# Earlier norm transposes, earlier weights, rotation before value split and stacked queries by transfer in a one-core encoder layer

## The chip, the cores and the metric

The kernel runs on one core of a Trainium2 chip. The metric is the device time of one launch in microseconds, over a few runs. A profile is one execution on the chip. In it PE is TensorE's matrix multiplication, PEld its weight load, DVE the vector engine, ACT the scalar engine, POOL GpSimd, and SP the engine that does nothing but issue transfers. A "q" behind an engine's name is its sequencer, where it issues transfers or waits. "L269" is line 269 of the kernel before.

## The reference

One encoder layer over 1024 tokens of width 1024. Two kinds of attention share one input norm and one input projection:

```python
hn = rmsnorm(h, norm_mix)
proj = hn @ w_in                      # 1024 x 2304
qa, ka, va, qb, kb, vb = split(proj)  # A: 8 query heads, 2 key/value heads; B: 8 heads
qa, ka = partial_rope(qa, cos, sin), partial_rope(ka, cos, sin)   # 16 of 64 dims
o_a = window_gqa_sink(qa, ka, va, sink)       # |i-j| <= 128, a learned sink
o_b = neighbourhood_attention(qb, kb, vb, rpb)  # 8 x 16 window on a 16 x 64 grid
mix = concat(rmsnorm(o_a, norm_a), rmsnorm(o_b, norm_b))
h = h + mix @ w_out
hn = rmsnorm(h, norm_ffn)
h = h + (silu(conv3(hn @ w_gate) + conv_b) * (hn @ w_up)) @ w_down
return rmsnorm(h, norm_final)
```

The change touches only the first norm, the projection's first tiles, the rotation and the layout of group A's queries.

## The kernel before

Everything lies transposed: features on the 128 partitions, the 1024 tokens along the row. Matrix products are made nearly exact by splitting each operand into a high part and the rest: one 128 x 128 block of weights against 512 tokens takes three matmuls (`block`, L171 to L174). Weights are loaded raw, ACT rounds them to the high part (`halve_w`, L156), and DVE, or POOL in some stages, subtracts to get the low part (L157).

The input projection has 18 tiles of 128 columns, made in the order m = 0 to 17. Tiles 0 to 5 belong to group A in two groups of three: the first tile of a group (m = 0 and 3) holds a 64-row key head and its 64-row value head, the two others hold four query heads. The tiles 0 and 1 (`first`) are computed straight from the incoming input, the third (m = 2, `third`) behind them from its own weights. The input is used without its norm: each product is scaled by the row factor `rstd1` when it leaves PSUM (`evacuate`, L269).

`rstd1` is made so: ACT squares the eight input tiles and DVE adds them into `acc` (L211, L213). `inverse_power` turns 4 blocks of `acc` on PE (L221), DVE sums them (L223), scales and adds epsilon (L224), and POOL raises to the power of minus one half (L225). `widen` (L263) turns the result back on PE, broadcast over the partitions, and ACT copies it out (L772). This is done once for each half of the tokens. In between lie the scans: ACT sums the squares of the eight output weight tiles (`scan_out`, L755 and L756), which are needed for a scale much later.

After the evacuation, `turn` treats a group A tile. `rotate` (L277 to L292) sends the rows to be rotated out by two transfers, one from ACT and one from SP, into a folded layout (L285), does four DVE operations (L287 to L289) and sends the rows back by two SP transfers (L291). For a group's first tile, `split_v` also takes the largest absolute value of each value row (L357), forms scales from it (L358 to L362), and makes two half precision parts, the high one on ACT (L374), the rest on DVE (L375); these are then turned by a transposing transfer (L378).

`stacks` then builds the operands of the score products, two tiles a and b each with a high part in one half of the partitions and a rest in the other. There are two ways for queries. `split_first` (L305) computes every quarter in its place: two ACT operations (L309) and two DVE operations (L310), each on 64 rows. `split_pair` (L294) computes the high part of all 128 rows at once on ACT (L297) and the rest on DVE (L299), and three SP transfers of 64 rows bring them across (L300 to L302), the third of which overwrites rows that the first reads. `split_first_k` does the keys of the first group with L316 to L319. Before the change the first group's two query tiles both use `split_first`, the second group's both use `split_pair`.

The attention itself works in units of 128 queries. For each head PE makes scores (L432), DVE adds the mask and finds the maximum (L462), ACT takes the exponential (L466), and the result is turned, partly by PE (L494, copied out by L497 and L498), partly by a transposing transfer (L488, a flip), and multiplied with the values (L521). Between these steps PE works on the remaining projection tiles: `rest` is a generator that gives one block at a time, and `fill(n)` takes n of them. `FILL0 = 22` blocks, the 16 of the fourth tile and 6 of the fifth, come ahead of the first score.

What sets the order of the work:

- PE is scheduled by hand: its instructions run in the order in which the program writes them.
- On DVE, ACT, POOL and SP a planner lays out the order from when an instruction becomes ready in its own model and from its place in the program. `tc.high_priority(offset=...)` moves a passage up. `behind(name)` puts what is written in it behind a marked instruction of the same engine. Once laid out, each engine serves its queue strictly in order.
- The stacks of the first two tiles are written behind "copied", the evacuation of the fourth tile's first half. The fifth tile's second half of weights is written behind "stack" (the last ACT half of the second tile's stacks), with its low part on POOL. The third tile's stacks come behind those weights.
- Tiles come from pools with a fixed number of slots. Raw weights have two slots, so a load waits until an earlier raw tile was halved.

In `turn` the order of the two calls and the name of the loop variable matter:

```python
g, i = divmod(m, 3)
if i == 0:
    (v,), up = split_v(t, slice(64, 128))
    va[g] = v
    for i in range(2):
        scaled_gain(2 * g + i, up, C_NA + 2 * g + i)
rotate(t, 64 if i == 0 else 128, ["back"] * (m in (1, 2)))
```

## Time and profile before

| what | value |
|---|---|
| median of 3 runs | 1039.76 us (1037.07 to 1040.96) |
| span of the profiled execution | 1035.9 us; its time outside the span is not given |
| PE busy | 1011.7 us, 98% |
| DVE busy | 880.0 us, 85% |
| ACT busy | 679.3 us, 66% |
| POOL busy | 214.1 us, 21% |
| PE clock granted | 0.997 of full speed |
| first matmul of the input product / first score | 5.45 us / 62.29 us |

The profile's rows give a start, a duration and an instruction as "output <- inputs". A bracket at the end tells how long the engine was idle ahead of it and which instruction or transfer ended that. Matmuls overlap, so the time of one matmul is best read from the distance between two starts, not from its duration. The view of busy time by stretches gives, for each engine, busy microseconds and the number of instructions.

### The profile page before, as it was taken

To read this page: it belongs to the slowest core of one execution; us is meant where nothing else is said; L and a number is where in the kernel's file an instruction comes from. 1 tells how busy PE (TensorE), PEld (TensorE's weight loads), DVE (VectorE), ACT (ScalarE), POOL (GpSimd) and SP (SyncE) were. 2 spreads that over 40 slices of the span, in tenths; PEclk is the share of its full clock that TensorE was granted. 3 is DMA by queue.
4 is the path that set the end of the run, shared out by engine and by line. 5 is a ranking of instruction groups with operands and counts; after the bars stand their busy time and mean duration, and the time that the engine had idled before them with its cause. 6 is when DMAs were issued, how large, how long until landed. Compare 5 with 4: busy or idle time off the path is not lost.

```text
span 1035.9 us, 15696 instructions
## 1 busy us (share of the span) xinstructions
PE 1011.7 (98%) x5102; PEld 577.3 (56%) x5102; DVE 880.0 (85%) x1748; ACT 679.3 (66%) x1243; POOL 214.1 (21%) x341
## 2 busy tenths in 40 slices
PE   9998999999999999999999999999999999999996
PEld 7776777777775545544444444444444444444446
DVE  6699998766898699899898988888888879899875
ACT  8567787767687587645777777754535656655551
POOL 2235455676866301000000000000000000000002
PEclk9999999999999999999999999999999999999998
DMA  9447473676689775300687867733232778878744
GB/s 347 155 98 149 109 139 83 151 168 140 134 180 224 213 276 193 121 1 21 222 266 261 276 241 250 251 111 133 82 112 102 240 252 297 301 250 264 255 153 163
DMA packets 144275, 191.28 MB, mean 185 GB/s; under 512 B 77376, under 2 KB 88640, under 8 KB 144192
## 3 DMA queue, kind: packets, MB, share of 16 engines
q1 hardware_dynamic: 133536, 164.51, 54.7%
q10 hardware_dynamic: 10656, 25.76, 6.4%
q8 instruction: 40, 0.66, 0.2%
q14 instruction: 43, 0.35, 0.1%
HBM read 132.81 MB, written 28.57 MB: 156 GB/s over the span
## 4 chain that ended last, share of the span: by engine, by line
PE 71%; DVE 6%; ACT 1%; DMA 1%; issue 1%; POOL 0%; ACTq 0%; DVEq 0%; SPq 0%; POOLq 0%
PE dn L1177 6%; PE dn L1178 6%; PE dn L1176 6%; PE pj L180 6%; PE z L1176 5%; PE z L1177 5%; PE z L1178 5%; PE y L1176 4%; PE y L1177 4%; PE y L1178 4%; PE x L1176 4%; PE x L1177 4%; PE x L1178 3%; PE pj L172 2%; PE pj L174 2%; PE pj L173 2%
## 5 line engine op out<-in xcount | busy, mean ns | idle before, releaser
L1178 PEld LDWEIGHTS <-wlo 128*128 128x128 f16 x898 | 87.9, 98 | 101.3 <-DVE wlo L1151 0.2
L1176 PEld LDWEIGHTS <-whi 128*128 128x128 f16 x898 | 88.1, 98 | 100.3
L1177 PEld LDWEIGHTS <-whi 128*128 128x128 f16 x898 | 87.9, 98 | 100.3 <-issue 0.2
L1178 PE MATMUL dn<-xd,wlo 128*128 128x512 f16 (+1 forms) x330 | 120.4, 365 | 0.0
L1177 PE MATMUL dn<-xd,whi 128*128 128x512 f16 (+1 forms) x330 | 120.4, 365 | 0.0
L1176 PE MATMUL dn<-xd,whi 128*128 128x512 f16 (+1 forms) x330 | 120.4, 365 | 0.0
L172 PE MATMUL pj<-xgh,whi 128*128 128x512 f32 x248 | 106.8, 431 | 0.8 <-ACT whi L156 0.8
L1177 PE MATMUL z<-hg,whi 128*128 128x512 f16 x264 | 100.1, 379 | 0.0
L1178 PE MATMUL z<-hg,wlo 128*128 128x512 f16 x264 | 100.1, 379 | 0.0
L1176 PE MATMUL z<-hg,whi 128*128 128x512 f16 x264 | 100.1, 379 | 0.0
L466 ACT ACTIVATE p<-p,nm 128x385 f32<-128x385 f32 (+3 forms) x128 | 74.8, 585 | 38.0 <-DVE nm L462 33.3
L174 PE MATMUL pj<-xgh,wlo 128*128 128x512 f32 x248 | 97.9, 395 | 1.4 <-POOL wlo L157 1.4
L173 PE MATMUL pj<-xgl,whi 128*128 128x512 f32 x248 | 97.5, 393 | 0.0
L1150 ACT ACTIVATE whi<-ws,m 128x512 f16<-128x512 f32 (+1 forms) x96 | 65.9, 709 | 35.6 <-DVE ws L1317 19.5
L1151 DVE SCALAR_TENSOR_TENSOR wlo<-ws,m,whi 128x512 f16<-128x512 f32 (+1 forms) x96 | 70.2, 741 | 17.8 <-ACT whi L1150 17.6
L1031 POOL TENSOR_TENSOR back<-back,cst 128x4 f32<-128x4 f32 (+1 forms) x7 | 2.8, 396 | 356.7 <-DVE back L1030 356.7
L1165 ACT ACTIVATE scan<-scan 128x1024 f32<-128x1024 f32 (+1 forms) x60 | 61.1, 1019 | 17.0 <-DMA scan<-in_w_down_dram 12.3
L1150 ACT ACTIVATE whi<-raw,m 128x512 f16<-128x512 f32 (+1 forms) x78 | 51.4, 700 | 17.9 <-DMA raw<-in_w_down_dram 12.7
L1151 DVE SCALAR_TENSOR_TENSOR wlo<-raw,m,whi 128x512 f16<-128x512 f32 (+1 forms) x78 | 55.4, 732 | 7.5 <-ACT whi L1150 6.9
L1176 PE MATMUL y<-hg,whi 128*128 128x512 f16 x160 | 60.6, 379 | 0.0
L1177 PE MATMUL y<-hg,whi 128*128 128x512 f16 x160 | 60.6, 379 | 0.0
L1178 PE MATMUL y<-hg,wlo 128*128 128x512 f16 x160 | 60.6, 379 | 0.0
(291 smaller groups left out, 2465.5 us busy)
## 6 DMA issues: line engine op xcount, KB each, us to landing
xd<-x SPq DMA_DIRECT2D x77, 256.0 KB, 5.4
raw<-in_w_down_dram SPq DMA_DIRECT2D x64, 256.0 KB, 3.8
x<-c ACTq DMA_DIRECT2D x22, 512.0 KB, 3.5
scan<-in_w_gate_dram SPq DMA_DIRECT2D x18, 512.0 KB, 4.7
scan<-in_w_up_dram SPq DMA_DIRECT2D x18, 512.0 KB, 4.3
raw<-in_w_gate_dram SPq DMA_DIRECT2D x18, 512.0 KB, 3.8
raw<-in_w_up_dram SPq DMA_DIRECT2D x18, 512.0 KB, 4.4
raw<-in_w_in_dram SPq DMA_DIRECT2D x32, 256.0 KB, 3.1
```

The lines of the kernel that those rows point to most:

```text
L172: nc.tensor.matmul(ps, w[0], x[0][:, tsl(h)], start=first, stop=False)
L173: nc.tensor.matmul(ps, w[0], x[1][:, tsl(h)], start=False, stop=False)
L174: nc.tensor.matmul(ps, w[1], x[0][:, tsl(h)], start=False, stop=last)
L180: nc.tensor.matmul(ps, a, b, start=i == 0 and b is x[h][0] and a is w[0], stop=i == len(ws) - 1 and a is w[1])
L466: nc.scalar.activation(p[:, 0:e], p[:, 0:e], AF.Exp, bias=nm, scale=-1.0, accum_out=sm)
L1031: nc.gpsimd.tensor_tensor(back, back, unit_back.to_broadcast([128, n]), op=ALU.mult)
L1150: mark["whi"] = nc.scalar.activation(hi, src, AF.Copy, scale=by)
L1151: nc.vector.scalar_tensor_tensor(lo, src, by, hi, op0=ALU.mult, op1=ALU.subtract)
L1165: nc.scalar.activation(t, t, AF.Square, accum_out=dst)
L1176: nc.tensor.matmul(ps, w[0], x[0], start=first and i == 0, stop=False, skip_group_check=True)
L1177: nc.tensor.matmul(ps, w[0], x[1], start=False, stop=False, skip_group_check=True)
L1178: nc.tensor.matmul(ps, w[1], x[0], start=False, stop=last and i == len(ws) - 1, skip_group_check=True)
```

## The change

Four edits, all of them in the first 60 us of the program:

```diff
         def turn(m, t):
             g, i = divmod(m, 3)
             if i == 0:
+                rotate(t, 64)
                 (v,), up = split_v(t, slice(64, 128))
                 va[g] = v
                 for i in range(2):
                     scaled_gain(2 * g + i, up, C_NA + 2 * g + i)
-            rotate(t, 64 if i == 0 else 128, ["back"] * (m in (1, 2)))
+            else:
+                rotate(t, 128, ["back"] * (m in (1, 2)))
 
         def stacks(m, t):
...
-                qa[g, i - 1] = split_pair(t) if g else split_first(t)
+                qa[g, i - 1] = split_first(t) if m == 1 else split_pair(t)
...
         ps3 = [bank("s", "s") for _ in range(2)]
-        for _ in product(ps3[0], third.w, xg, 0):
-            pass
...
+        jobs[1].load()
+        jobs[1].load_rest()
         for d in range(KT):
             scan_out(d)
...
         rstd1 = big("rstd1", "rstd")
-        vs1 = [inverse_power(acc[:, tsl(h)], D, "pt") for h in range(2)]
-        rest3 = product(ps3[1], third.w, xg, 1)
-        for _ in range(3):
-            next(rest3)
-        for h in range(2):
-            nc.scalar.activation(rstd1[:, tsl(h)], widen(vs1[h], "pt"), AF.Copy)
+        rest3 = (step for h in range(2) for step in product(ps3[h], third.w, xg, h))
+        next(rest3)
+        v1 = gains
+        with tc.high_priority(offset=300):
+            for h in range(2):
+                sums1 = bank("st", "pt")
+                for c in range(4):
+                    nc.tensor.transpose(sums1[:, c * 128:(c + 1) * 128], acc[:, h * HALF + c * 128:h * HALF + (c + 1) * 128], ident)
+                nc.vector.tensor_reduce(v1[:, 4 * h:4 * h + 4], sums1[:, :].rearrange("p (c w) -> p c w", w=128), axis=mybir.AxisListType.X, op=ALU.add)
+            nc.vector.tensor_scalar(v1, v1, 1.0 / D, EPS, op0=ALU.mult, op1=ALU.add)
+            nc.gpsimd.tensor_tensor(v1, v1, minus_half[:, 0:1].to_broadcast([128, 8]), op=ALU.pow)
+            for _ in range(5):
+                next(rest3)
+            for h in range(2):
+                mark["root"] = nc.scalar.activation(rstd1[:, tsl(h)], widen(v1[:, 4 * h:4 * h + 4], "pt"), AF.Copy)
         for p, ps in zip(first, banks):
             p.t = tmp("t")
             for h in range(2):
                 evacuate(p.t, ps[h], h, False)
-            if p is first[0]:
-                jobs[1].load()
-                jobs[1].load_rest()
```

In words: both halves of the third tile's product become one stream of 16 steps. One step is written ahead of the norm's eight transposes, five between them and the widening, ten after; before it was eight ahead and three between. The two halves of the norm share one scaling, one power over eight columns and one buffer (`gains`, used later for something else). The fourth tile's two weight loads and their halving are written ahead of the scans. In `turn`, a group's first tile is rotated before its values are split, and over 64 rows. The third tile's query stacks are built by `split_pair`.

## The prediction

> **What bounds the kernel now.** I read the page first, then the busy time by stretches, then the timeline of each engine from 23 to 86 us, the list of waits, and the views of single lines.
>
> The span, and busy time by stretch (columns: PE, PEld, DVE, ACT, POOL, then granted clock, DMA share, GB/s):
>
> ```profile
> span 1035.9 us, 15696 instructions
> ```
>
> ```profile
> 50.00:75.00 25.00, 22.85 (x104) 18.38 (x104) 23.71 (x56) 14.18 (x27) 6.58 (x13) 1.00 0.38 94
> 75.00:100.00 25.00, 22.29 (x126) 16.33 (x125) 23.31 (x68) 19.09 (x48) 12.89 (x25) 1.00 0.76 150
> 100.00:125.00 25.00, 24.66 (x148) 18.85 (x146) 23.37 (x82) 19.34 (x51) 14.13 (x31) 1.00 0.53 120
> ```
>
> PE carries the kernel: from 100 us on it idles a third of a microsecond in 25. Before that, between 50 and 100 us, it is idle 4.9 us of 50 while DVE is busy 47. So there are two things to win: PE's waits themselves, and DVE work that now stands in front of PE. The order of PE's instructions is written by hand, so a microsecond taken out of PE's stream early moves all that follows, unless something else is late there. The order on DVE, ACT, POOL and SP is laid out by the planner from priorities and readiness.
>
> The waits, in PE's timeline (start, duration, instruction, idle before it and who ended it):
>
> ```profile
> 30.05 0.39 PE L172 MATMUL s<-xgh,whi 128*128 128x512 f32 x1
> ...
> 35.27 0.39 PE L174 MATMUL s<-xgh,wlo 128*128 128x512 f32 x1
> 35.50 1.03 PE L221 MATMUL st<-cst,sq 128*128 128x128 f32 x8
> 36.29 0.48 PE L172 MATMUL s<-xgh,whi 128*128 128x512 f32 x1
> ...
> 38.21 0.39 PE L174 MATMUL s<-xgh,wlo 128*128 128x512 f32 x1
> 39.03 0.65 PE L263 MATMUL sw<-cst,v 128*128 128x128 f32 x4 [0.43 <-POOL v L225]
> 40.70 0.65 PE L263 MATMUL sw<-cst,v 128*128 128x128 f32 x4 [1.01 <-POOL v L225]
> 41.10 0.47 PE L172 MATMUL s<-xgh,whi 128*128 128x512 f32 x1
> ...
> 57.99 0.39 PE L174 MATMUL pj<-xgh,wlo 128*128 128x512 f32 x1
> 59.15 0.50 PE L172 MATMUL pj<-xgh,whi 128*128 128x512 f32 x1 [0.78 <-ACT whi L156]
> 59.49 0.39 PE L173 MATMUL pj<-xgl,whi 128*128 128x512 f32 x1
> 61.26 0.50 PE L174 MATMUL pj<-xgh,wlo 128*128 128x512 f32 x1 [1.38 <-POOL wlo L157]
> ...
> 62.29 0.28 PE L432 MATMUL s<-ka,q 128*128 128x256 f32 x1
> ...
> 64.21 0.35 PE L432 MATMUL s<-ka,q 128*128 128x256 f32 x1
> ```
>
> From the first to the second row are 23 steps in 5.22 us: 0.227 us a matmul, 0.68 us a block of three. Measured from start to start, the four waits cost 0.82 - 0.23 = 0.6 (39.03), 1.67 - 0.40 = 1.27 (40.70; four widening transposes take 41.10 - 40.70 = 0.40), 1.16 - 0.23 = 0.93 (59.15) and 1.77 - 0.23 = 1.54 (61.26): 4.3 us. The first step behind a wait is longer too (59.49 - 59.15 = 0.34, 0.11 over), 0.4 for four. So **4.7 us** are lost before the first score matmul at 62.29. Counted forward it is the same: 114 matmuls of 0.227 and 16 transposes of 0.1 from 30.05 end at 57.5.
>
> **Part 1, the norm.** What feeds the widening now, from the timelines of DVE, POOL and ACT, and two views of lines with the power (count, then shortest, median, longest in ns):
>
> ```profile
> 28.09 2.54 DVE L213 TENSOR_TENSOR sq<-sq 128x1024 f32<-128x1024 f32 x2
> 36.13 1.29 DVE L223 TENSOR_REDUCE v<-st 128x4 f32<-128x512 f32 x2 [5.50 <-PE st L221]
> ...
> 42.02 0.69 DVE L269 TENSOR_TENSOR t<-pj,rstd 128x512 f32<-128x512 f32 x1 [0.97 <-ACT rstd L772]
> ```
>
> ```profile
> 35.59 0.99 POOL L554 TENSOR_TENSOR xb<-cst,rr 128x384 f32<-128x384 f32 x1 [9.72 <-DMA rr<-in_rpb_dram]
> 37.64 1.34 POOL L225 TENSOR_TENSOR v<-v,minus_half 128x4 f32<-128x4 f32 x1 [1.07 <-DVE v L224]
> ```
>
> ```profile
> L880 POOL TENSOR_TENSOR wo_by<-owm,minus_half x1: 580/580/580, 205.3 to 205.3; 128x1 f32<-128x1 f32 x1
> ```
>
> ```profile
> L225 POOL TENSOR_TENSOR v<-v,minus_half x6: 1017/1027/1566, 37.6 to 361.0; 128x4 f32<-128x4 f32 x6
> ```
>
> ```profile
> 34.75 1.14 ACT L156 ACTIVATE whi<-raw 128x512 fp32r<-128x512 f32 x2
> ```
>
> The sum of squares is done at 28.09 + 2.54 = 30.63, but its transposes stand behind 24 matmuls, so DVE sat idle 5.50 us. After the change they stand behind three: PE reaches them at 30.05 + 0.68 = 30.73, just after the sum. The eight transposes now span 36.29 - 35.50 = 0.8 us; both reduces are done near 32.5, the one tensor_scalar at 32.7. The power goes from four columns to eight: one column takes 0.58, four 1.03, so 0.15 a column more and about 1.63 for eight (ends: one power of four, 1.03, and two of the slowest, 3.13). That ends at 34.4 (33.8 to 35.9). PE needs it after five more blocks, 31.5 + 3.4 = 34.9. I take no wait; the far end makes it 1.0.
>
> ACT's last scan and the two copies L156 end at 34.75 + 1.14 = 35.9 in any order among themselves, so rstd1 comes at 36 to 37 and both evacuations of the first tile are done near 37.5 instead of 42.7. PE's third product ends at 30.05 + 48 x 0.227 + 1.6 = 42.5. The evacuations are thus hidden under PE's blocks: what they gain is room on DVE.
>
> **Part 2, the weights ahead of the scans.** Two loads and four half operations move, none is added. Now their DVE halves fill DVE's idle time before 40 us; with evacuations from 36.5 they must be gone by then. SP takes the two loads ahead of eight scan loads; nothing but a scale at 200 us waits for the scans. Cost nothing; if they stayed late, 1.4 us of DVE would fall between the evacuations, still under PE's blocks until 42.5.
>
> **Part 3, rotation ahead of the value split.** In the code before, the loop `for i in range(2)` in `turn` overwrites `i`, so the test `i == 0` behind it fails, and the first and fourth tile are rotated over all 128 rows, value rows included. Their transfers back (L291) write rows that the split (L375) still reads:
>
> ```profile
> 50.02 1.28 DVE L375 SCALAR_TENSOR_TENSOR vhl<-t,down,vhl 64x1024 f16<-64x1024 f32 x1
> ```
>
> ```profile
> 51.33 3.17 SPq L291 DMA_DIRECT2D t<-f  x4
> ```
>
> ```profile
> 54.13 1.06 ACT L316 ACTIVATE ka<-t 64x1024 fp32r<-64x1024 f32 x1 [5.55 <-DMA t<-f]
> ```
>
> L291 leaves at 51.33, 0.03 after L375 ends (51.30); SP serves in order, so the second and third tile's transfers back stand behind it, and ACT idles 5.55. After the change 64 rows are rotated, the split touches none of them, and the transfers leave after the last rotation add. An instruction's time goes by its columns, so the rotation's four DVE operations stay as long. First tile: evacuated 37.5, transfers out, four operations, back: K stacks possible from about 45 instead of 54.13. What is late next is the code's own order: the stacks' DVE halves are queued behind the evacuation of the fourth tile's first half, and PE gives that at 42.5 + 24 x 0.227 = 48.0, done 48.9. So of the 9 us on ACT some 6 reach DVE, and the early ACT halves bring the fifth tile's second weight half (ACT L156, then POOL L157, queued behind them) well ahead of PE's need. The two waits at 59.15 and 61.26 go, 2.5 us. For the fourth tile the same freedom is worth nothing: its stacks are used eight units later.
>
> **Part 4, the third tile's stacks by transfers.** `split_first` costs two ACT and two DVE operations of 64 rows, `split_pair` one of each over 128 rows and three transfers:
>
> ```profile
> 57.60 2.46 DVE L310 SCALAR_TENSOR_TENSOR q<-t,q 64x1024 fp32r<-64x1024 f32 x2
> ...
> 60.82 2.71 DVE L310 SCALAR_TENSOR_TENSOR q<-t,q 64x1024 fp32r<-64x1024 f32 x2
> ...
> 63.57 0.48 DVE L462 CUSTOM_DVE_ANT_0 p<-s,cst,nsink 128x256 f32<-128x256 f32 x1
> ...
> 66.86 1.22 DVE L357 TENSOR_REDUCE top<-t 64x1 f32<-64x1024 f32 x1
> ```
>
> ```profile
> L297 ACT ACTIVATE q<-t x2: 1042/1045/1048, 89.2 to 108.5; 128x1024 fp32r<-128x1024 f32 x2
> L300 SPq DMA_DIRECT2D q<-q x2: 462/523/584, 90.2 to 110.2; - x2
> L299 DVE SCALAR_TENSOR_TENSOR t<-t,q x2: 1224/1225/1226, 90.6 to 109.7; 128x1024 fp32r<-128x1024 f32 x2
> ```
>
> ```profile
> L302 SPq DMA_DIRECT2D q<-t x2: 466/786/1106, 94.0 to 113.4; - x2
> ...
> DMA to landing us min/median/max: 3.7/4.0/4.4
> ```
>
> DVE saves 2.71 - 1.22 = 1.5 and ACT 1.1. DVE's work is then 48.9, two K halves of 1.2, one L310 pair of 2.46, one evacuation of 0.69, L299 of 1.22: 55.7. The last transfer, L302, leaves with the next SP slot, 55.8 to 56.3, and lands 4.0 later: 60.1 (59.5 to 60.7). PE's first score comes at 62.29 - 4.7 = 57.6, the third, the first that reads these stacks, 64.21 - 62.29 = 1.92 behind it: 59.5. So PE waits 0.6 there (0 to 1.2). Behind that wait stand PE's next blocks and scores, and DVE, which has the fourth tile's value reduction (L357) to fill it. SP's own queue: the three transfers stand ahead of the sixth tile's weight loads and the fourth tile's rotation, half a microsecond each by L300's row.
>
> Against this part speaks the Trainium skill, "DMA: Bandwidth & Descriptors", section "Anatomy of one DMA": about 2.0 us fixed for each transfer plus its bytes at 436 GB/s, so 2.6 us for these 256 KB, an estimate from that page. The row has 3.7 to 4.4 for the same size, so the page's price is too low here; by the page the stacks would stand at 58.7 and the 0.6 would be nothing.
>
> **DVE's new room.** With PE at its first score at 57.6 and DVE done at 55.7, DVE is no longer late: at present its first softmax (63.57) starts the moment L310 ends (60.82 + 2.71 = 63.53), 0.9 after the scores. The 2 us between go to what now stands at 66.86 and after, the fourth tile's reduction and rotation, and these are what PE waits for at 80:
>
> ```profile
> 80.19 0.44 PE L494 MATMUL pt<-cst,p 128*128 128x128 f32 x2 [1.31 <-DVE turned L498]
> ```
>
> That wait I expect to go (ends: 0 to 1.3, and up to 2.7, PE's whole idle time between 75 and 100).
>
> **The sum.** -4.7 (four waits) + 0.6 (third score) - 1.3 (L494) = -5.4 us. Ends: -3.5 (third score 1.2, L494 stays) to -7.4 (no wait there, all idle time to 100 us gone). After 100 us nothing in the change acts directly; but the planner lays out other engines anew, and a changed order can cost or give waits like the one at 80.19; for two of them I add 2.5 to both sides. The profiled execution has a span of 1035.9 and what lies around it is not on the page; the three timed runs are 1037.07 to 1040.96, so 1.2 to 5.1 above it. I take the difference over to the median: 1039.76 - 5.4 = 1034.4. The forecast's own range is 1029.9 to 1038.8. Half a per cent, 5.2 us, is about what a measurement of this kernel can tell from no change, and the forecast sits on it.
>
> **Rivals.**
>
> *POOL's queue takes the gain of the norm.* POOL ran the bias tile L554 at 35.59, ahead of the power, when its load had landed. If the planner keeps that order, the power starts at 35.59 + 0.99 = 36.6 and ends at 38.2, and PE, in place of 1.9 us in two waits, has one of 38.2 - 34.9 = 3.3: the gain falls from 5.4 to 2.1: 1037.7 (1039.0 if the wait at 80.19 stays as well). For it: the row at 35.59, and one instruction cannot be passed in a queue. Against: the power now becomes ready at 32.7, about 3 us before that load landed, and has the priority. The Trainium skill, "TensorE: Matmul & The Clock Gate", section "What's actually happening", says that a pause of about 3.4 us halves the clock; no pause quoted here is longer than 1.6, and the granted clock is 1.00 in the rows above, so this trace cannot show it. By that rule this rival would lose another 1.7 us of gain, an estimate (3.4 us at half speed).
>
> *The stacks come late: slower.* The third tile's ACT half ran at 59.01 (the second L309 pair):
>
> ```profile
> 59.01 2.12 ACT L309 ACTIVATE q<-t 64x1024 fp32r<-64x1024 f32 x2
> ```
>
> If it stays there, because its rotation's transfers back are still late on SP, the chain L297, L300, L302 needs about 1.0 + 0.5 + 3.3 + 0.5 + 4.0 = 9.3 us (its 3.3 an estimate, L302 leaving 94.0 - 90.2 = 3.8 after L300): PE's third score at 68.3 instead of 64.21, 4.1 late, and all scores behind it: 1043.9; with a flip or a weight load ahead of L302 on SP, another 1.5, 1045.4. It decides from L297 starting after 64.21 - 9.3 = 54.9. Against: rotation of the third tile can start when PE's third product ends, 42.5 instead of 41.10 + 15 x 0.227 = 44.5, and nothing then holds SP; I get 51.
>
> *The gain is given back later.* From 100 to 340 us PE and DVE are both nearly full (the rows above: DVE 23.4 of 25). If DVE, not PE, sets the pace there and a new order costs it two waits of 1.3, the gain is 2.8 and the time 1037.0. For it: DVE's share; against: PE's idle 0.34 of 25.
>
> *The change does not act:* if the planner puts the stacks' ACT halves behind the same transfers as now, only the norm's 1.9 us are left: 1037.9.
>
> **How the numbers follow.** Forecast 0.72, POOL's queue 0.08, stacks late 0.08, given back 0.10, no action 0.02. Of the forecast's own range (1029.9 to 1038.8, middle 1034.4) somewhat over half lies below 1039.76 - 5.2 = 1034.56: 0.55 of 0.72 is 0.40, and 0.02 comes from the cases in which a rival's loss is met by a better order later: 0.42 faster. Slower than 1044.96 are the upper end of the late stacks (0.05), a new order that hits several waits at once (0.05): 0.10. The remainder, 0.48, is no change. Range: 1029.9 to 1039.5, which takes in the forecast and the three cases of a smaller gain and leaves out the late stacks and the tails, some 0.2.
>
> **What would show it.** In the new profile: the transposes L221's counterpart on PE at 30.7 and no wait at L263; first evacuation near 36.5; L291 near 42 and the first K stack's ACT half near 45; the weight waits at the fifth tile gone and its product unbroken; first score at 57.6; one ACT and one DVE operation of 128 rows for the third tile, the third score within 1.2 us of its turn; no 1.3 us wait for L498 near 75. Wrong if PE waits over 1 us at L263 (POOL's order), or at its third score (stacks), or if PE reaches 100 us of its old count early by 5 us and the end is early by less than 3 (given back).

## The result and the profile after

| | before | after |
|---|---|---|
| median of 13 runs each, us | 1038.97 (1037.07 to 1041.33) | 1037.12 (1035.60 to 1038.05) |
| ratio | | 0.9983, 95% interval 0.9975 to 0.9991 |
| span of the profiled execution, us | 1035.9 | 1035.1 |
| PE busy, us | 1011.7 | 1012.4 |

The change makes the kernel 0.17% faster (0.09 to 0.25%), 1.8 us where 5.4 had been forecast. The time lies within the range, the size of the gain does not fit its working.

One thing first for reading the two traces side by side. The third tile's first matmul, ahead of which the change touches nothing on PE, starts at 30.58 in the new profile and at 30.05 in the old. The 0.53 us between them are taken here as not the change's and are subtracted from the PE times of after: e2 below, which changes nothing ahead of that matmul either, has it at 30.69.

The busy time by stretches of after (columns as in the prediction):

```profile
span 1035.1 us, 15696 instructions
```

```profile
50.00:75.00 25.00, 20.50 (x89) 16.57 (x88) 22.03 (x50) 14.79 (x26) 5.73 (x10) 0.93 0.58 127
75.00:100.00 25.00, 23.63 (x133) 18.23 (x132) 20.74 (x66) 17.65 (x45) 12.78 (x26) 1.00 0.72 141
```

Between 50 and 75 us PE is idle 4.5 us, where it was 2.15 before, and the granted clock is 0.93, where it was 1.00. The PE timeline of after says where:

```profile
30.58 0.39 PE L172 MATMUL s<-xgh,whi 128*128 128x512 f32 x1
...
31.27 1.03 PE L776 MATMUL st<-cst,sq 128*128 128x128 f32 x8
...
35.57 1.03 PE L263 MATMUL sw<-cst,gains 128*128 128x128 f32 x8
...
58.66 0.28 PE L434 MATMUL s<-ka,q 128*128 128x256 f32 x1
...
60.27 0.39 PE L174 MATMUL pj<-xgh,wlo 128*128 128x512 f32 x1
65.01 0.55 PE L434 MATMUL s<-ka,q 128*128 128x256 f32 x1 [4.35 <-DMA q<-t]
...
65.57 0.63 PE L172 MATMUL pj<-xgh,whi 128*128 128x512 f32 x1
66.00 0.63 PE L173 MATMUL pj<-xgl,whi 128*128 128x512 f32 x1
...
69.71 0.33 PE L434 MATMUL s<-ka,q 128*128 128x384 f32 x1
```

No bracket stands at the widening (35.57) or in the fifth tile's product, and the first score starts at 58.66 instead of 62.29. All of that is lost again at one place: the third score, the first to read the stacks made by transfers, waits 4.35 us for a transfer into `q`. Behind it a block's matmuls follow each other by 0.43 us (65.57, then 66.00), not by 0.23: PE runs at half its clock for about 3 us. In slices, the granted clock is the third figure from the right:

```profile
64.00:66.00 2.00, 0.99 (x3) 0.93 (x4) 1.90 (x5) 0.00 (x1) 1.25 (x3) 0.65 0.16 35
66.00:67.00 1.00, 1.00 (x4) 0.80 (x3) 0.91 (x6) 0.41 (x1) 0.37 (x3) 0.50 0.66 130
...
68.00:69.00 1.00, 1.00 (x6) 0.84 (x6) 1.00 (x1) 0.36 (x2) 0.00 (x0) 0.98 0.95 246
```

The sum of the whole, by the starts of the same matmuls in both timelines and with the 0.53 taken off: the first score is 4.16 us early (62.29 + 0.53 - 58.66). The third score is 0.27 late (65.01 - 64.21 - 0.53): the wait took 4.43. From the third score to the first one over 384 keys are 4.70 us (69.71 - 65.01); in the kernel before they were 3.30 (that score starts at 67.51 there): 1.40 for the clock. Then the new kernel catches up. PE's idle time from 75 to 100 us falls from 2.71 to 1.37, and by the row at 99.54 (99.18 before) 1.84 us are back. Up to 336.56 (335.62) another 0.58 is lost, and then a wait for a flip is gone, which the kernel before has in this row:

```profile
339.07 0.38 PE L596 MATMUL o<-turned,v 128*128 128x256 f16 x2 [1.77 <-DMA turned<-stage]
340.95 0.38 PE L596 MATMUL o<-turned,v 128*128 128x256 f16 x2
```

```profile
336.56 0.49 PE L598 MATMUL o<-turned,v 128*128 128x256 f16 x4
...
340.22 0.38 PE L598 MATMUL o<-turned,v 128*128 128x256 f16 x2
```

From there on after is 1.26 us ahead (340.95 + 0.53 - 340.22), and so it stays to the end (1035.9 + 0.53 - 1035.1 = 1.33): -4.16 + 4.43 + 1.40 - 1.84 + 0.58 - 1.67 = -1.26. Without the flip's 1.67 us this execution would be 0.41 us late: the gain left in the trace is the flip's, for which the change was not costed. Nor does it come with the change's parts: between 330 and 345 us PE idles 0.11 us in after and nothing in f4 below, but 0.7 to 1.9 us in every other trace.

Why the stacks are late shows in the timelines of DVE, ACT, POOL and SP:

```profile
43.66 1.21 DVE L289 TENSOR_TENSOR f<-f 64x256 f32<-64x256 f32 x1
44.80 1.00 DVE L287 TENSOR_TENSOR f<-f,turns 128x128 f32<-128x128 f32 x2
...
50.91 0.49 DVE L287 TENSOR_TENSOR turns<-turns 128x128 f32<-128x128 f32 x2 [1.73 <-DMA turns<-t]
...
52.25 0.68 DVE L269 TENSOR_TENSOR t<-pj,rstd 128x512 f32<-128x512 f32 x1
...
55.21 3.45 DVE L310 SCALAR_TENSOR_TENSOR q<-t,q 64x1024 fp32r<-64x1024 f32 x2
...
59.30 1.22 DVE L299 SCALAR_TENSOR_TENSOR t<-t,q 128x1024 fp32r<-128x1024 f32 x1
```

```profile
55.07 1.06 ACT L297 ACTIVATE q<-t 128x1024 fp32r<-128x1024 f32 x1
```

```profile
43.33 1.26 POOL L556 TENSOR_TENSOR xb<-cst,rr 128x384 f32<-128x384 f32 x1 [3.66 <-DMA rr<-in_rpb_dram]
44.55 1.10 POOL L557 TENSOR_TENSOR xb<-cst,rr 128x256 f32<-128x256 f32 x1
...
55.23 2.35 POOL L157 TENSOR_TENSOR wlo<-raw,whi 128x512 fp32r<-128x512 f32 x1 [8.27 <-ACT whi L156]
```

```profile
57.60 0.36 SPq L150 DMA_DIRECT2D raw<-in_w_in_dram  x1
58.07 0.51 SPq L300 DMA_DIRECT2D q<-q  x1
59.41 0.65 SPq L285 DMA_DIRECT2D f<-t  x1
60.54 0.51 SPq L301 DMA_DIRECT2D q<-t  x1
62.06 0.47 SPq L302 DMA_DIRECT2D q<-t  x1
```

DVE gives the low half (L299) at 59.30 + 1.22 = 60.5. The last transfer, L302, leaves at 62.06, and PE goes on at 65.01. By the list of SP's waits, L302 stood 1.0 us until the first transfer, L300, whose rows it overwrites, had landed. L300 itself had left only at 58.07, 1.9 us after its ACT half (L297) ended, behind a weight load (L150) for which SP waited 1.5 us until POOL's L157 was done. Three readings are possible: DVE is late, SP's queue holds the transfers back, or the halved clock is the real loss. And if DVE is late: is it because POOL works beside it? L289 takes 1.21 here, and 0.41 in the kernel before, while POOL's L556 and L557 run; the pair L310 takes 3.45, in the kernel before 2.46, while POOL's L157 runs.

### The profile page after: what moved, and what is told of

The parts are those of the page before. It is cut to its first block, busy times and chain, and to the rows that moved or that the text cites. A ratio compares the mean times of both kernels' runs of the same rounds, so it can differ in the third digit from the quotient of the medians.

```text
span 1035.1 us, 15696 instructions
## 1 busy us (share of the span) xinstructions
PE 1012.4 (98%) x5102; PEld 578.9 (56%) x5102; DVE 880.2 (85%) x1746; ACT 678.2 (66%) x1242; POOL 214.5 (21%) x340
## 4 chain that ended last, share of the span: by engine, by line
PE 71%; DVE 6%; DMA 2%; ACT 1%; issue 1%; POOL 0%; DVEq 0%; ACTq 0%; POOLq 0%
PE pj L180 6%; PE dn L1186 6%; PE dn L1184 6%; PE dn L1185 6%; PE z L1184 5%; PE z L1186 5%; PE z L1185 5%; PE x L1184 4%; PE y L1184 4%; PE y L1186 4%; PE x L1186 4%; PE y L1185 4%; PE x L1185 4%; PE pj L172 2%; PE pj L174 2%; PE pj L173 2%
```

## The experiments

The theory after the result: the third tile's DVE half comes some 4 us later than costed, in large part because POOL's operations with two operands slow DVE's, and the chain of transfers behind it adds its latency; the first three parts give what was forecast. Rivals: SP's order of transfers is the cause; the halved clock is; or the first three parts gained less than the first score suggests. Where a kernel lists its edit against another one, that is named. All were timed beside the kernel before, whose median was 1038.39, 1038.43 and 1038.59 in the three batches.

| kernel | median, us | ratio to before (95%) | first / third score / first over 384, us |
|---|---|---|---|
| before | 1038.97 | | 62.29 / 64.21 / 67.51 |
| after | 1037.12 | 0.9983 (0.9975 to 0.9991) | 58.66 / 65.01 / 69.71 |
| e1_in_place | 1036.03 | 0.9974 (0.9965 to 0.9983) | 58.54 / 63.58 / 68.46 |
| e2_transfers_alone | 1042.67 | 1.0039 (1.0025 to 1.0054) | 62.85 / 70.18 / 74.96 |
| e3_ahead_on_sp | 1040.25 | 1.0013 (1.0004 to 1.0023) | 58.53 / 65.05 / 70.85 |
| e4_kept_busy | 1039.10 | 1.0003 (0.9993 to 1.0012) | 58.46 / 68.27 / 71.59 |
| f4_kept_busy_16 | 1036.78 | 0.9986 (0.9977 to 0.9996) | 58.06 / 65.33 / 68.63 |
| f1_back_first | 1034.35 | 0.9967 (0.9956 to 0.9977) | 58.33 / 62.70 / 66.02 |
| f2_no_pool | 1034.38 | 0.9962 (0.9950 to 0.9975) | 58.86 / 60.72 / 63.96 |
| f3_both | 1033.52 | 0.9962 (0.9950 to 0.9975) | 58.34 / 60.20 / 63.44 |
| g1_transfers_quiet | 1037.06 | 0.9983 (0.9974 to 0.9991) | 58.37 / 62.91 / 66.23 |
| g2_norm_as_before | 1036.65 | 0.9981 (0.9973 to 0.9990) | 60.46 / 62.53 / 65.85 |
| g3_rotation_as_before | 1037.77 | 0.9993 (0.9984 to 1.0001) | 60.47 / 62.56 / 65.88 |
| g4_weights_as_before | 1036.51 | 0.9980 (0.9969 to 0.9991) | 60.40 / 63.67 / 66.92 |

The score times come from the PE timeline of each profile; the third tile's first matmul starts between 30.42 and 31.21 us in the new kernels' traces, so that a few tenths between them mean little. Ratios are the safer comparison between batches.

### Part 4 undone, and part 4 alone

e1_in_place is the new kernel with the third tile's stacks built in place, as before:

```diff
-                qa[g, i - 1] = split_first(t) if m == 1 else split_pair(t)
+                qa[g, i - 1] = split_pair(t) if g else split_first(t)
```

> The changed kernel with one part undone: the third tile's query stacks are computed in place again (two ACT and two DVE operations of 64 rows, no transfers); the norm, the weights and the rotation stay changed. Theory A (the stacks' transfers cost the gain): PE reaches the first score near 58.7 as in the changed kernel, the third score follows within 2 us without a wait, the clock stays at 1.00 between 60 and 70 us, and the end comes 4 to 6 us before the kernel before: ratio 0.994 to 0.996. Theory B (DVE sets the pace between 75 and 340 us, whatever the start): the early gain is given back by 100 us and the end is 0.5 to 2 us early: ratio 0.998 to 0.9995, no better than the changed kernel.

e2_transfers_alone is the kernel before with that line changed the other way and nothing else.

> The kernel before with only the third tile's stacks built by transfers. Theory A: PE waits 3 to 5 us at its third score, the clock halves for about 3 us behind that, some of it is regained before 100 us: 1 to 4 us slower, ratio 1.001 to 1.004. Theory B (what is lost or won before 75 us does not reach the end): within 1 us of the kernel before, ratio 0.999 to 1.001.

Alone, part 4 costs 0.39% (0.25 to 0.54), 4 us, and the cost stands at the forecast place, the third score of e2:

```profile
70.18 0.55 PE L432 MATMUL s<-ka,q 128*128 128x256 f32 x1 [5.30 <-DMA q<-t]
```

The way there leads through SP's queue. DVE's half (L299) ends at 62.85, but L302 leaves only at 67.09: SP's waits have 2.8 us for POOL's L157, which held a weight load ahead of L300, and another 2.8 us in which L302 waited for L300 to land.

Taking part 4 out of the new kernel gains only 0.9 us by the ratios, and the intervals of e1 and after overlap. The ratio of 0.9974 lies between what the two theories had expected. The PE and DVE timelines of e1 say why:

```profile
63.58 0.36 PE L434 MATMUL s<-ka,q 128*128 128x256 f32 x1 [2.52 <-DVE nm L464]
...
64.22 0.63 PE L173 MATMUL pj<-xgl,whi 128*128 128x512 f32 x1
64.65 0.63 PE L174 MATMUL pj<-xgh,wlo 128*128 128x512 f32 x1
```

```profile
55.55 3.56 DVE L310 SCALAR_TENSOR_TENSOR q<-t,q 64x1024 fp32r<-64x1024 f32 x2
...
59.87 2.45 DVE L310 SCALAR_TENSOR_TENSOR q<-t,q 64x1024 fp32r<-64x1024 f32 x2
```

PE was ready at 63.58 - 2.52 = 61.06. The second pair L310 gives the stacks at 59.87 + 2.45 = 62.3, 1.3 us too late. The bracket names `nm`, the softmax of the first score, which ends at 63.43; scores have two PSUM banks (the kernel's pool has two slots for each kind), so the third writes where the first was read from. That softmax stands on DVE behind the second pair L310 and an evacuation. Even without any transfer DVE is thus too late for the third score, by its stacks and by what is queued behind them, and the clock falls here too (0.43 us from 64.22 to 64.65). So the transfers are part of the loss, and DVE's lateness is a cause of its own.

### SP's order

e3_ahead_on_sp is the new kernel with nothing queued on SP between the third tile's transfers, and the two that need DVE written in the other order:

```diff
+            if early:
+                nc.sync.dma_start(f32(a[64:128, :]), t[0:64])
-            nc.sync.dma_start(f32(b[64:128, :]), t[64:128])
-            nc.sync.dma_start(f32(a[64:128, :]), t[0:64])
+            mark["crossed"] = nc.sync.dma_start(f32(b[64:128, :]), t[64:128])
+            if not early:
+                nc.sync.dma_start(f32(a[64:128, :]), t[0:64])
...
-                qa[g, i - 1] = split_first(t) if m == 1 else split_pair(t)
+                qa[g, i - 1] = split_first(t) if m == 1 else split_pair(t, m == 2)
...
-                with behind(*["stack", "low"] * (m == 3)):
+                with behind(*["stack", "low", "crossed"] * (m == 3)):
...
-                    with behind(*["stack"] * (i == 1)):
+                    with behind(*["stack", "crossed"] * (i == 1)):
```

> The changed kernel, with the sixth tile's weight loads and the fourth tile's rotation transfers queued on SP behind the stacks' transfers, and the transfer that the third score needs ahead of the one that the fourth needs. Theory C (SP's queue makes the stacks late): the first of the three transfers leaves near 56.2 instead of 58.07, and the third score's wait falls from 4.4 us to under 1.5, with no drop of the clock: 3 us better than the changed kernel. Theory D (the DVE half, which ended at 60.5, makes them late): the wait falls by 0.5 to 1 us only, to 3.3 to 3.9, and the end is within 1 us of the changed kernel.

The SP timeline of e3 shows that the queue was cleared: the transfers leave 0.03 and 0.6 us after L299 has ended (59.16 + 1.22 = 60.38), where after's left at 60.54 and 62.06. The other order did not come about: the transfer that the third score needs, L302, still leaves second.

```profile
60.41 0.49 SPq L303 DMA_DIRECT2D q<-t  x1
60.99 0.55 SPq L302 DMA_DIRECT2D q<-t  x1
```

```profile
65.05 0.55 PE L437 MATMUL s<-ka,q 128*128 128x256 f32 x1 [4.50 <-DMA q<-t]
```

PE still goes on at 65.05: the last transfer leaves 1.07 us sooner and takes 4.06 us until PE moves, instead of 2.95. For the new kernel the queue theory falls. The whole is even 0.30% slower than after by the two ratios, 3.1 us, of which 1.1 stand at the first score over 384, since the clock stays at 0.50 up to 70 us; the rest comes later, presumably from the sixth tile's weights and the fourth tile's rotation, which now leave later.

### The clock

e4_kept_busy and f4_kept_busy_16 are the new kernel with 36 and 16 spare matmuls ahead of the third score, whose results nothing reads:

```diff
+                    if (g, b, j) == (0, 0, 2):
+                        spare = bank("spare", "o")
+                        for _ in range(36):
+                            nc.tensor.matmul(spare[:, 0:128], ones, ones, start=True, stop=True)
```

> The changed kernel with 36 extra matmuls of 128 columns into an unused bank ahead of the third score, about 4 us that lie in PE's wait; their result is thrown away. It separates the wait from the halved clock behind it. Theory E (the clock falls because PE pauses over 3.4 us, and costs 1.4 us): the third score stays near 65.0, the granted clock stays 1.00 from 64 to 68 us, and PE is 1 to 1.5 us ahead of the changed kernel at 70 us. Rival (the slow matmuls behind the wait come from the transfers' traffic or from the inputs, not from the pause): PE is at 70 us where the changed kernel is, or later. At the end either may be hidden by the waits before 100 us: 0 to 1.5 us better.

> The changed kernel with 16 extra matmuls of 128 columns ahead of the third score in place of the 36 of the earlier experiment, which took 9 us and pushed the score itself back by 3.3. At 0.25 us apiece 16 take 4 us and fit into the wait of 4.4. Theory E (the pause halves the clock, which costs 1.4 us): third score at 65.0 as in the changed kernel, granted clock 1.00 from 64 to 68 us, and PE 1.2 to 1.5 us ahead of the changed kernel at 70 us; at the end 0 to 1.4 better. Rival: no difference at 70 us.

The 36 took 8.20 us, longer than the wait, so the third score came 3.3 us later than after's. But the clock stays at 1.00, and the distance to the first score over 384 is 3.32 (71.59 - 68.27), that of the kernel before, against 4.70 in after. The halved clock costs 1.4 us in after. With 16 (3.73 us, then 0.87 of wait) the third score comes 0.32 later than after's and the one over 384 is 1.08 earlier. Of that nothing certain reaches the end: 0.9986 against 0.9983, intervals overlapping. The clock is a real but small loss. The trace of f4 gives the 1.08 us back from 75 to 100 us: PE idles 1.95 us there, in after 1.37, and the clock is 0.93.

### DVE's lateness: two causes taken away

f1_back_first is e1 with the third tile's rotation queued behind both of the first tile's transfers back, so that these leave together:

```diff
+            if p.m == 0:
+                mark["back0"] = mark["back"]
...
-            with behind("turned"):
+            with behind("turned", "back0"):
```

> The stacks in place again (as in the first experiment), and on SP the third tile's outgoing rotation transfer is queued behind both of the first tile's transfers back; before, the second of these left 3.2 us after the first (48.05 after 44.90). Theory F (SP's order holds the first stacks): ACT's first key half starts near 48 instead of 50.2, DVE's stacks end 1.5 to 2.5 us sooner, and PE's wait at the third score falls from 2.7 to about 0.7: 1 to 2 us better than the first experiment. Rival: DVE's own order, with the third tile's rotation ahead of the stacks, holds them anyway: the wait stays over 1.8 us and the end is within 0.7 us of the first experiment.

f2_no_pool is e1 with POOL's work moved away from DVE's: the bias tiles L556 and L557 later, the fifth tile's second low half on DVE itself:

```diff
-            nc.gpsimd.tensor_tensor(gains[:, i:i + 1], col(c), up, op=ALU.mult)
+            mark["gain"] = nc.gpsimd.tensor_tensor(gains[:, i:i + 1], col(c), up, op=ALU.mult)
...
-            nc.gpsimd.tensor_tensor(xv[:, 1:4], mk, view(-1, 1, 3), op=ALU.subtract)
-            nc.gpsimd.tensor_tensor(xv[:, 0::4], far, view(-1, 2, 2), op=ALU.subtract)
+            with behind("gain"):
+                nc.gpsimd.tensor_tensor(xv[:, 1:4], mk, view(-1, 1, 3), op=ALU.subtract)
+                nc.gpsimd.tensor_tensor(xv[:, 0::4], far, view(-1, 2, 2), op=ALU.subtract)
...
-                        mark["early"] = True
+                        mark["early"] = False
```

> The stacks in place again, and POOL kept idle while DVE rotates and stacks: the two early bias tiles are queued behind the fourth tile's gains, and the low half of the fifth tile's second weights is made on DVE (0.68 us there) instead of POOL. Theory G (POOL's operations slow DVE's operations that read two SBUF operands): the rotation add of the first tile, 1.21 us in the changed kernel and 0.41 in the kernel before, falls back to about 0.4, the stack operation of 2.21 falls to 1.22, DVE's stacks end about 2 us sooner, and PE's wait at the third score falls from 2.7 to under 1.2: 1 to 3 us better than the first experiment. Rival (these were long for another reason, a wait inside them): their times stay, and with 0.68 more on DVE the wait grows to over 3 us.

f3_both has both edits.

> Both edits of the two experiments beside it, on the version with the stacks in place. If the causes add, PE's wait at the third score is gone (under 0.5 us), the clock stays at 1.00 between 60 and 70 us, PE is 3.5 us ahead of the kernel before at 70 us, and the end is 2.5 to 4 us early: ratio 0.9955 to 0.9975. If DVE sets the pace up to 100 us whatever comes before, the lead falls to 1.5 us or less there, and the ratio is 0.998 or more.

DVE and PE in f2, from their timelines:

```profile
44.27 0.41 DVE L289 TENSOR_TENSOR f<-f 64x256 f32<-64x256 f32 x1
44.60 0.48 DVE L287 TENSOR_TENSOR f<-f,turns 128x128 f32<-128x128 f32 x2
...
53.28 2.46 DVE L310 SCALAR_TENSOR_TENSOR q<-t,q 64x1024 fp32r<-64x1024 f32 x2
...
57.09 2.47 DVE L310 SCALAR_TENSOR_TENSOR q<-t,q 64x1024 fp32r<-64x1024 f32 x2
59.60 0.48 DVE L464 CUSTOM_DVE_ANT_0 p<-s,cst,nsink 128x256 f32<-128x256 f32 x1
```

```profile
58.86 0.28 PE L434 MATMUL s<-ka,q 128*128 128x256 f32 x1
...
60.72 0.28 PE L434 MATMUL s<-ka,q 128*128 128x256 f32 x1
```

With POOL silent the rows that were long in after are back at 0.41, 0.48 and 2.46, although DVE now does 0.68 us of POOL's work as well, and the wait at the third score is gone altogether. That POOL's operations beside DVE are one cause of the late stacks is shown; how much is theirs alone is not. In e1 they lengthen L288 (1.23 instead of 0.41), L157 (0.91 instead of 0.69) and the first pair L310 (3.56 instead of 2.46), 2.1 us together. But DVE also waits only 0.52 us for the third tile's transfer (`turns`) in f2, against 1.93 in e1, and why that transfer comes sooner was not tried. Against e1, f2's ratio is lower by 0.0012, though the intervals overlap; at the score over 384 it is 4.5 us ahead. f1 leaves POOL alone and keeps a wait of 2.36 us at the third score; it comes 0.9 us sooner there than e1 and its clock does not fall, and so it is 2.4 us ahead of e1 at the score over 384. That is its rival's expectation (a wait over 1.8 us, an end within 0.7 us of e1), since by the ratios f1 gains 0.07% on e1, which is not clear of noise. f3 has the lowest median, but its ratio is that of f2, 0.38% (0.25 to 0.50) below the kernel before, 4.0 of the 5.4 us that were forecast: what f1's edit adds to f2's does not show at the end. f3's third score follows the first by 1.86 us, as if there were no stacks to wait for.

### Each part alone, against f3

Four kernels undo one part each in f3, where no other wait covers it. In g1 the third tile's stacks come by transfers again; g2 has the norm of before, g3 the `turn` of before, g4 the fourth tile's weights behind the first evacuations, each by the lines of the change's own diff.

> The version with both edits (POOL kept idle, the first tile's transfers back ahead), but with the third tile's stacks by transfers as in the changed kernel. It asks whether the prediction's step for the transfers was right once DVE is on time. Theory D' (the transfers need over 3.5 us after DVE's half, and DVE's half cannot end before 57.5): PE still waits 2 to 3 us at its third score, where the version with stacks in place waits 0, and the end is 1 to 3 us later than that version. Rival (only DVE's delay made them late): the wait is under 1.2 us, as the prediction had it, and the end is within 0.7 us of that version.

> The version with stacks in place and both edits, with the norm's transposes where they were in the kernel before. If the norm's part is worth what PE's waits there were (1.9 us): PE waits 1.5 to 2 us at the widening again, its first score comes 1.5 to 2.5 us later, DVE has less room before it, and the end is 1.5 to 3 us later than with the norm changed. Rival (DVE's room is what counts, and the waits before 100 us swallow the rest): within 0.7 us of it.

> The same version with the rotation behind the value split and over 128 rows, as in the kernel before. If the rotation's transfers back, held by the split, are what made the first stacks late: the key half on ACT starts 3 us or more later, the weights behind it are late again, PE waits 1 to 3 us at the fifth tile or at the first scores, and the end is 1 to 4 us later. Rival (the stacks are held by DVE's order in any case): within 0.7 us.

> The same version with the fourth tile's weights written behind the first evacuations, as in the kernel before. The prediction costed this part at nothing: within 0.7 us of the version. Rival: the two halves fall between the evacuations (1.4 us on DVE), the fourth tile's product starts late on PE, and the end is 1 to 2.5 us later.

g1 is the cleanest trial of part 4: DVE undisturbed, the stacks by transfers. Its rows on DVE, SP and PE:

```profile
49.05 0.69 DVE L269 TENSOR_TENSOR t<-pj,rstd 128x512 f32<-128x512 f32 x1 [0.66 <-PE pj L174]
...
56.24 0.68 DVE L157 TENSOR_TENSOR wlo<-raw,whi 128x512 fp32r<-128x512 f32 x1
56.84 1.22 DVE L299 SCALAR_TENSOR_TENSOR t<-t,q 128x1024 fp32r<-128x1024 f32 x1
```

```profile
58.82 0.59 SPq L302 DMA_DIRECT2D q<-t  x1
```

```profile
62.91 0.36 PE L434 MATMUL s<-ka,q 128*128 128x256 f32 x1 [2.53 <-DVE f L288]
```

The bracket names a DVE operation that has nothing to do with the score; what the score needs is L302, issued at 58.82, and 4.1 us later PE runs. The third score is 2.7 us later than in f3 (62.91 against 60.20). By the ratios g1 is 0.21% slower, 2.2 us (the median of f3 comes from another batch and five runs, so the ratios are the safer measure). So part 4 loses even here, though the two intervals touch (0.9974 and 0.9975): DVE's half ends at 58.06 and the chain behind it takes 4.9 us to PE, while PE needs the stacks at 60.20.

g2, g3 and g4 each bring the first score 2.1 us later, and by the ratios they cost 0.19, 0.31 and 0.18%, or 2.0, 3.2 and 1.9 us; only g3's interval lies clear of f3's, the two others overlap its edge. In g2 PE waits at the widening for 0.3 us only, where 1.5 to 2 had been expected; in g3 the key half on ACT starts 2.1 us later than in f3 (48.99 against 46.91), where 3 or more had been expected. Each of the three has a wait for the fifth tile's weights, of 1.0, 1.7 and 1.8 us. In g4's PE timeline:

```profile
59.22 0.50 PE L174 MATMUL pj<-xgh,wlo 128*128 128x512 f32 x1 [1.79 <-DVE wlo L157]
```

Behind this wait g4's clock is 0.52 from 60 to 62 us, and the third score follows the first by 3.27 us instead of f3's 1.86: 1.4 us more. Undoing any one part in f3 brings the wait back, so the parts do not add up: there all three are needed to have the fifth tile's weights in time.

What stays open: the end does not follow from the score times alone. f1, g1, g2 and g3 have their first score over 384 within 0.4 us of each other (65.85 to 66.23), yet their ratios lie between 0.9967 and 0.9993. Some 2 to 3 us are decided behind 70 us. The traces put them next to it: from 75 to 100 us PE idles 2.02 us in f1, 3.19 in g2, 4.09 in g1 (with the clock at 0.93) and 4.85 in g3, in the order of the ratios. Most of that is waits for the softmax chain on DVE, ACT and POOL; which order on those engines makes them was not tried. The profiled execution of g1 took 1039.89 us, its median is 1037.06, so its rows there may be longer than usual.

## Why the prediction was wrong

**Part 1, right.** The transposes were forecast at 30.73 and start at 31.27 - 0.53 = 30.74, the power over eight columns at 1.63 (POOL's L779 took 1.66), no wait at the widening (none), the first evacuation near 36.5 (36.84 - 0.53 = 36.31). POOL's queue took nothing: L556 first ran at 38.00, after the power had ended at 35.21. g2 puts the part's worth at the first score at 2.1 us; forecast were 1.9 and its share of the first steps behind waits. In g2 these 2.1 us stand in part at the fifth tile's weights, so the size agrees better than the place.

**First score, right.** 4.7 us early were forecast, 4.16 came. The rest is 0.3 us of idle ahead of the row at 57.63 and a slower step behind it.

**Part 3, right in what it frees, wrong in when.** The waits at the fifth tile's weights went. But the first K stack's ACT half, forecast near 45, ran at 50.18 (L316). The text held that nothing holds SP once the rotation comes ahead of the split. The third tile's own transfer out (L285) did: it stood on SP at 47.44, ahead of the first tile's second transfer back (48.05). f1, with these two exchanged, has L316 at 48.10, and f3 at 46.91.

**The step that failed: part 4's "DVE's work is then 48.9, ... 55.7. The last transfer, L302, ... lands 4.0 later: 60.1", and so "PE waits 0.6 there (0 to 1.2)".** Measured: L299 ends at 60.5, 4.3 us after the forecast's 55.7 + 0.53, and PE waits 4.35, with 1.4 for the clock on top. Four things were left out. One: the third tile's own rotation stands ahead of the evacuation at 48.9 in DVE's queue, and its transfer came late, so that DVE idled 1.73 us with its work behind it; the evacuation ended at 52.93. Two: POOL's operations lengthened DVE's, L289 by 0.80, L287 by 0.52 and L310 by 0.99 us; the prediction counted quiet durations. A sign of it stood in its own rows: the second pair L310 of the kernel before took 2.71 us, the first 2.46, and POOL's L157 ran there from 59.18 to 61.21. Three: the low half has 1.1 us of rotation (L287 to L289) before it even where nothing is late. Four: L302 did not leave with the next SP slot but 1.5 us after L299, held by the landing of L300; e3 shows that this alone did not decide. g1, without POOL's part, has its evacuation done at 49.74, which is the forecast's 48.9 moved by g1's own 0.66 (30.71 against 30.05) to within 0.2, and its L299 still ends 1.7 us later than the forecast's 55.7 moved in the same way, by the rotation and 0.68 for the weights. The latency of the transfer was right: 4.1 from L302 to PE in g1 and e3, 2.95 in after, for a forecast of 4.0. The section of the Trainium skill that the prediction weighs against this step ("DMA: Bandwidth & Descriptors", "Anatomy of one DMA") is headed as the path of transfers that GpSimd issues; these are issued by SP, and nothing in the sum rests on it.

**The rival "the stacks come late".** Its mechanism is what happened. It was to decide from L297 starting after 54.9; L297 started at 55.07, which is 54.54 with the 0.53 taken off. Its chain was costed at 9.3 us and took 65.01 - 55.07 = 9.94, so that the third score came at 64.48 against 64.21 before. So the deciding point was right within 0.6 us: the kernel stood near it, and came out even there instead of the 4.1 us late of the priced case, in which L297 stays at 59.01. This rival had 0.08 and was the better account of the place. Its condition hung on DVE's and SP's queues, which the prediction had not followed through to the third tile.

**DVE's new room, right in the sign for a wrong reason.** The wait at L494 went, and PE's idle time from 75 to 100 us fell by 1.34, as the 1.3 of the sum had it. But the traces point to PE's own lateness as the reason: in f3, where PE is 4 us early, that stretch again has 3.03 us of idle, more than before. In part the rival "given back later" is true as well: PE's lead of 4 us in f3 at 70 us is one of 3.6 at the end, while f4's 1.1 us against after is lost.

**Part 2, sized at nothing, is worth about 2 us** once the others are in place (g4). Without it the fourth tile's halvings fall between the evacuations (DVE's L157 at 37.98 and 39.94 in g4), what follows on DVE is later, and the fifth tile's weights come late. "Still under PE's blocks" was worked out for the fourth tile alone.

**What the sum did not hold.** 1.67 us of the gain come from a flip at 339 us that no longer waits. The prediction had allowed 2.5 us to either side for such things and could not say which. So far as the gain in the trace is this flip's, it is luck.

By the clock rule that the prediction cites from the Trainium skill ("TensorE: Matmul & The Clock Gate", section "What's actually happening"), a pause of about 3.4 us halves the clock. The pause of 4.35 us agrees; e1's fell after 2.52 us (and 0.24 shortly before) and g4's after 1.79 us, which the measurement shows and the rule does not. The same section of the Trainium skill says that the window runs free of the kernel, which may be why 2.36 (f1), 2.53 (g1) and 1.69 us (g3) left the clock at 1.00; no run here tests that.

## What to carry to other kernels

When a step is moved onto an engine with an in-order queue, write out everything that stands ahead of it in that queue in the new kernel, the moved tile's own earlier steps among them, with the transfers that those wait for; the sum "work after the last known point" leaves them out. Replacing engine work by transfers needs a consumer that is far away: here 1.5 us of DVE were exchanged for a chain of 4.9 us right in front of PE, while the same helper is used without a wait of PE for tiles needed eight units later. A transfer that overwrites rows which an earlier one reads also waits for that one to land. And before DVE work is counted at its quiet duration, see what POOL does beside it.

## What the runs showed of the hardware

- POOL operations with two operands and DVE operations with two operands in SBUF hold each other up as if one port served one at a time. In after the pair L310 takes 3.45 us instead of 2.46 beside POOL's L157, which lasts from 55.23 to 57.58: the first L310 takes its usual 1.2, the second waits and ends 1.1 us after POOL. L289 takes 1.21 instead of 0.41 beside L556, and POOL's own L556 and L557 1.26 and 1.10 instead of 0.99 and 0.71. The Trainium skill, "SBUF — State Buffer", section "SBUF: two separate sides", states such an exclusive lock: whichever of the two engines starts first holds the shared ports for its whole instruction. The trace agrees. What had not been expected is the price, an operation of 0.41 us lengthened to three times that.
- A halved clock cost 1.4 us after a pause of 4.35 us in after (4.70 against 3.32 us for the same matmuls) and 2.5 us after 4.50 us in e3 (5.80), where it lasted longer.
- The same transfer of 64 rows by 1024 took 2.95 to 4.1 us from its issue to the matmul that waits for it, and in e3 sending it 1.07 us sooner did not bring it sooner. The longer times stand where a transfer of the same size had left about 0.6 us ahead of it (e3, g1), the shorter one where that was 1.5 us (after).
